# Selection rounds traced behind RWKV pairs, put-away tiles spread, the last two v tiles ordered by output block

## The chip, the cores and the metric

The kernel runs on one core of a Trainium2 chip. The metric is the device time of one execution in microseconds (us), lower is better. The core has five engines with instruction streams of their own: TensorE (PE, with its weight loads PEld), VectorE (DVE), ScalarE (ACT), GpSimd (POOL) and SyncE (SP), which issues most DMAs.

## The reference, cut to what matters

One layer over 384 tokens (128 sample tokens in 8 blocks of 16, and a prompt of 256), width 1024, float32:

```
x1 = norm and modulation of x, projected by W_in
rw = RWKV-7 over 16 heads        (kernel: 8 pairs of heads, R0 .. R7)
ix = sum over heads of relu(q_i . k_i) * w_i      (the indexer's scores)
keep = the 64 (prompt) best scores of each row; for the sample its own keys beside them
ds = attention over the kept keys only            (kernel: 4 quarters, D0 .. D3)
x2 = x1 + gated mix of rw and ds, through W_out
h  = norm of x2;  128 x 128 experts, 16 chosen for each of 8 heads
y  = x2 + gate * sum over chosen experts of  weight * gelu(h . u_e) * v_e
```

The expert layer at the end is done in two ways: the prompt's 256 tokens densely against all 16,384 experts, the 128 sample tokens by gathering the rows of the chosen experts only.

## The kernel before

The kernel is written on a tile framework. Instructions are traced in program order; a scheduler then sets the order on each engine from a simulated timeline, with the traced order as priority. Tiles come from pools by tag, each tag with a number of buffers; a tile waits for the release of the buffer that it takes, and a pool opened in space that another one held waits for all tiles of that one.

Front, up to about 740 us: the string ORDER (line 177) lists the units in traced order. I is the indexer, g and G gate units, R the RWKV pairs, D the attention quarters, M units of the modulation. For I, a pool "idx" is opened on the right side; `index` computes the indexer's projections and calls `index_s` (sample) and `index_p` (prompt, two tiles of 128 and 256 keys). Score tiles have the tag "isc" (2 buffers) in it. Their sums run on VectorE (L983, L987), after relu on ScalarE (L986, L1021). Then `select` runs its rounds on VectorE: 9 of them on 276 columns for the sample, 8 on 128 and 8 on 256 columns for the prompt, each a MAX8 (L964) and a MATCH_REPLACE8 (L965), and a mask is written (mks L1029 to L1034, mkp L992). When "idx" closes, the pool "dsa" is opened in its space (called ds); D, M and G units take their tiles from that, among them qx, the copy of a quarter's projections out of PSUM (L876). R units work in the pool "rw" (tags "y" and "sq2" among them).

Middle, 740 to 1330 us: the mix with W_out, the choice of experts, and the prompt's weights. G holds the weights of each expert tile's 128 experts for 256 tokens.

End: `dense_u(j)` multiplies the normed tokens by the u rows of expert tile j (in_puT), and writes gelu of it: the first 36 tiles with 8 products in full float32, the others with the operands split in high and low fp32r halves and 24 products. `dense_v(j)` reads the v rows (in_pv, 512 KB), splits them in a high and a low fp32r half (`split`: wh on ScalarE L227, wl on VectorE or GpSimd L231), weights the gelu tile on GpSimd (L1478), splits it likewise (Gh, Gl) and accumulates 12 products of 512 columns in four PSUM banks bx, cp, dx, dx (two token halves by two column halves). Every third tile is taken whole, without a split, except from n = 126 on. The u tiles are made ahead as far as there is room: 76 kept, 20 put away to DRAM (NB, tag gO, array Ad) and read back in `dense_v` (tag gB, L1472), 11 in buffers gA; the rest (21) are made inside the v loop, each as soon as fewer than 11 of the gA tiles are in use. The put-away tiles are j = 76 to 95. Meanwhile POOL issues 256 gathers (L1532) of u and v rows for the sample tokens, whose products VectorE sums. At the end `residual` multiplies each PSUM block by the gate (L1513) and adds x2 (L1514), then writes out.

Of the kernel before, what the change touches and what calls it, by code (L numbers as in the profile page):

```python
# [13 lines left out]
F32R = mybir.dt.float32r  # L14
# [159 lines left out]

PSB = {"mm": 2, "fx": 2, "bx": 1, "dx": 2, "cp": 1}
ALIAS = {"ix": "cp", "cs": "bx", "u": "fx"}
ORDER = "GGIggggRRDMMMGRMRDMRGMGMRMDGMMRRMGDMMMGGGMGGM"


N1, NW, NA, NB = 36, 76, 12, 20  # L180
SR, UR = (0.5, 0.4, 0.69), 0.5
S0, PH = 30, 4
WB, EB = (4, 4, 3), 5
UENG, VENG, GENG, VN = 'v', 'v', 'g', 3
SENG = 'gv'
# [7 lines left out]
class K:  # L193
# [684 lines left out]
    def index(self):  # L878
        nc = self.nc
        H = lambda t: t.rearrange("p i (h d) -> p i h d", d=64)  # L880
        kiT = self.t([128, NT], tag="kiT")
        W, n = self.win("ki")
        kt = self.t([72, NT], tag="kt")
        nc.scalar.activation(kt, self.tposp(W, 0, n, self.LT), AF.Copy)
        x = self.t([128, 3, 72], tag="qx")
        p = self.ps([128, 3, 72], tag="dx")
        for i in range(3):
            nc.tensor.transpose(p[:, i], kt[:, i * 128:(i + 1) * 128], self.ident[0:72, 0:72])
        nc.scalar.activation(x, p, AF.Copy)
# [12 lines left out]
        for u in range(2):  # L902
            x = self.t([128, 3, 256], tag="qx")
            self.nat3(f"qi{u}", x, 256)
            qr = self.t([128, 3, 4, 64], tag="qr")
            self.rope(qr, H(x), 0, 4)
            p = self.ps([128, 4, 128], tag="dx")
            for h in range(4):
                self.mm(p[:64, h], qr[:, 0, h], self.ident)
            nc.scalar.activation(qiTs[:, :, u * 4:u * 4 + 4].rearrange("p b h t -> p h b t"),  # L910
                                 p[:64].rearrange("p h (b t) -> p h b t", t=16), AF.Copy)
            p = self.ps([128, 2, 2, 128], tag="dx")
            for c in range(2):
                for i in range(2):
                    nc.tensor.transpose(p[:, c, i], qr[:, 1 + i, 2 * c:2 * c + 2].rearrange("p a b -> p (a b)"), self.ident)
            nc.scalar.activation(qiTp[:, u * 2:u * 2 + 2], p.rearrange("p c i t -> p c (i t)"), AF.Copy)
        self.mks = self.index_s(qiTs, kiT, wi[:, 0])
        self.mkp = self.index_p(qiTp, kiT, wi)

    def dsa_quarter(self, u):  # L920
        nc = self.nc
# [37 lines left out]
    def select(self, work, rounds):  # L959

        nc = self.nc
        for _ in range(rounds):
            m8 = self.t([128, 8], tag="m8", bufs=2)
            nc.vector.max(m8, work)  # L964
            nc.vector.match_replace(out=work, in_to_replace=m8, in_values=work, imm_value=MARK)  # L965

    def index_p(self, qiT, kiT, wi):
        nc = self.nc
        out = []
        for i in range(2):  # L970
            n = 128 * (i + 1)
            sc = self.t([128, 276], tag="isc", bufs=2)[:, :256]
            for par in range(2):
                pr = slice(64 * par, 64 * par + 64)
                for c0 in range(0, 4, 2):
# [11 lines left out]
                            nc.vector.scalar_tensor_tensor(sc[:, :n], rl[:, :n], w, sc[:, :n], op0=OP.mult, op1=OP.add)  # L987

            nc.vector.memset(sc[0:64, n - 64:n], -BIG)
            self.select(sc[:, :n], 8)  # L990
            mk = self.t([128, 256], BF16, tag="mkp", bufs=2, pool=self.hpool)
            nc.vector.tensor_scalar(mk[:, :n], sc[:, :n], MARK, -BIG, op0=OP.not_equal, op1=OP.mult)  # L992
            out.append(mk)
        return out

    def index_s(self, qiT, kiT, wi):
        nc = self.nc
# [14 lines left out]
        for b in range(8):  # L1012
# [3 lines left out]
            with self.tc.issue_after(self.wdma.ins):  # L1016
# [3 lines left out]
            rl = self.t([128, 272], tag="rel", bufs=2)  # L1020
            nc.scalar.activation(rl, p, AF.Relu)  # L1021
            self.mm(psc, LW[:, b].rearrange("p a b -> p (a b)"), rl, start=(b == 0), stop=(b == 7))
        sc = self.t([128, 276], tag="isc", bufs=2)
        nc.scalar.activation(sc[:, 0:272], psc, AF.Copy)

        nc.vector.memset(sc[:, 272:276], 3.0e38)
        self.select(sc, 9)
        mk = self.t([128, 384], BF16, tag="mks", pool=self.hpool)
        nc.vector.tensor_scalar(mk[:, 0:256], sc[:, 0:256], MARK, -BIG, op0=OP.not_equal, op1=OP.mult)  # L1029
        m2 = self.t([128, 16], tag="m2")  # L1030
        nc.vector.tensor_scalar(m2, sc[:, 256:272], MARK, -BIG, op0=OP.not_equal, op1=OP.mult)
        ob = self.t([128, 8], tag="ob8")
        nc.vector.tensor_scalar(ob, self.c["blk"], 1.0, BIG, op0=OP.subtract, op1=OP.mult)
        nc.vector.tensor_tensor(mk[:, 256:384].rearrange("p (b t) -> p b t", t=16), m2.unsqueeze(1).to_broadcast([128, 8, 16]),  # L1034
                                ob.unsqueeze(2).to_broadcast([128, 8, 16]), op=OP.min)
        return mk

    def attend_p(self, u, qT, kT, vn, obT):
        nc = self.nc
# [401 lines left out]
    def dense_u(self, j):  # L1441
# [8 lines left out]
        else:  # L1450
            uh, ul = (x.rearrange("p (k e) -> p k e", k=8) for x in self.split(u, UENG[j % len(UENG)]))
            hi, lo = self.h2p
            for k in range(8):
                self.mm(p, uh[:, k], hi[:, k], start=(k == 0), stop=False)
                self.mm(p, uh[:, k], lo[:, k], start=False, stop=False)
                self.mm(p, ul[:, k], hi[:, k], start=False, stop=(k == 7))
        off = NW <= j < NW + NB
        g = self.kept(j) if j < NW else self.t([128, 256], tag="gO" if off else "gA", bufs=2 if off else NA, pool=self.late)
        nc.scalar.activation(g, p, AF.Gelu_apprx_tanh)  # L1459
        if off:  # L1460
            nc.sync.dma_start(self.Ad[j - NW], g)
        return g

    def dense_v(self, j, g, out, n):
        nc = self.nc
        v = self.expert(self.I["pv"][j * 128:(j + 1) * 128])
        whole = n % VN == 0 and n < 126
        if not whole:
            vh, vl = self.split(v, VENG[j % len(VENG)])
        if NW <= j < NW + NB:  # L1470
            g = self.t([128, 256], tag="gB", bufs=2)
            nc.sync.dma_start(g, self.Ad[j - NW])  # L1472
        if j >= NW:
            q = (j - NW) % 4
            if q == 0 and j > NW:
# [3 lines left out]
        if whole:  # L1479
# [2 lines left out]
                    m = self.mm(out[i][b], g[:, i * 128:i * 128 + 128], v[:, b * 512:(b + 1) * 512], start=(n == 0), stop=False)  # L1482
            self.vdone.append(m.ins.name)
            return
        gh, gl = (self.t([128, 256], F32R, tag=tag, bufs=2) for tag in ("Gh", "Gl"))
        self.hilo(gh, gl, g, "v")
        for i in range(2):
            tok = slice(i * 128, i * 128 + 128)
            for q, (l, r) in enumerate(((gh, vh), (gh, vl), (gl, vh))):
                for b in range(2):  # L1490
                    m = self.mm(out[i][b], l[:, tok], r[:, b * 512:(b + 1) * 512], start=(n == 0 and q == 0),
                                stop=(n == 127 and q == 2))
        self.vdone.append(m.ins.name)

    def weights_back(self, j):

# [10 lines left out]
    def residual(self, i, parts, g, x1):  # L1507

        nc = self.nc
        y = self.ring()  # L1510
        for b in range(2):
            cols = slice(b * 512, b * 512 + 512)
            nc.vector.tensor_tensor(y[:, cols], parts[b], g[:, cols], op=OP.mult)  # L1513
            (nc.vector if i == 1 and b else nc.gpsimd).tensor_tensor(y[:, cols], y[:, cols], x1[:, cols], op=OP.add)  # L1514
            nc.sync.dma_start(self.O["y"][i * 128:(i + 1) * 128, cols], y[:, cols])

    def x1_rows(self, i):
# [40 lines left out]
    def run(self):  # L1558
        self.dense = False
        with ExitStack() as front:  # L1560
# [20 lines left out]
            with ExitStack() as s:  # L1581
                rw = self.open(s, "rw")
                self.pool = rw
                self.rwkv_head()
                ds, n = None, dict.fromkeys("RGD", 0) | {"M": 8}
                for x in ORDER:
                    if x == "I":
                        with ExitStack() as s2:
                            self.pool = self.open(s2, "idx", side="right")
                            self.index()  # L1590
                        ds = self.open(s, "dsa", side="right")
                        continue
                    self.pool = rw if x == "R" else ds
                    self.lo_pattern = "g" if x == "g" else "v"
# [39 lines left out]
                sn[0] -= 1  # L1634
                next(sparse, None)

        gs, todo = {}, list(range(NW, 128))
        for j in range(N1):
            self.dense_u(j)
            if j >= S0:  # L1640
# [10 lines left out]

        def ahead(n):
            un[0] += UR
            if todo and un[0] >= 1 and (todo[0] < NW + NB or todo[0] < NW + NB + NA - 1):
                un[0] -= 1
                u = todo.pop(0)
                gs[u] = self.dense_u(u)
# [13 lines left out]
        self.weights_back(NW)  # L1671
        self.g2 = self.modrow(5, "fx")

        self.vdone = []
        for n, j in enumerate(order):
            self.pace = self.vdone[n - 5] if n > 4 else None
            pull(SR[2])
            while todo and sum(u >= NW + NB for u in gs) < NA - 1:
                u = todo.pop(0)
                gs[u] = self.dense_u(u)  # L1680
            self.dense_v(j, gs.pop(j) if j >= NW else self.kept(j), out, n)
            if n == 122:
                for _ in sparse:
                    pass
                self.residual(0, [self.acc[:, b * 512:b * 512 + 512] for b in range(2)], self.gate2(0), self.x1_rows(0))
                g, x1 = self.gate2(1), [self.x1_rows(i) for i in (1, 2)]
        for i in range(2):
            self.residual(1 + i, out[i], g, x1[i])

# [24 lines left out]
```

## Time and profile before

| | us |
|---|---|
| median of 3 runs | 1815.54 (1814.88 to 1816.27) |
| profiled execution | 1820.84 |
| its span | 1819.1 |
| granted TensorE clock, mean | 0.969 |
| front (ORDER's units) | to about 740 |
| mix, choice, weights | about 740 to 1330 |
| v loop and its end | about 1330 to 1819 |

The profiled execution is one run and lies 5.3 us above the median. How its page is read: the busy rows show each engine's share in 40 slices of 45.5 us, in tenths; the row PEclk is the clock that TensorE was granted. A timeline row is start, duration, engine, line, operation, what it writes and reads, and in brackets the idle time ahead of it with what ended that.

### The profile page before, as it was taken

Reading aid. Unit: us, or ns where it says so; the run is one execution under the profiler, and the core shown is the slowest. Engines: PE = TensorE matmul, PEld = TensorE weight load, DVE = VectorE, ACT = ScalarE, POOL = GpSimd, SP = SyncE. Lnnn points to the kernel's source line nnn. Section 1 sums busy time; section 2 is a strip of 40 time slices with the busy share of each in tenths; the row PEclk is TensorE's granted clock in tenths of the full one; section 3 lists DMA queues with packets and bytes.
Section 4 is the critical chain, followed back from the end, with each engine's and each line's share of the span. In section 5 each row is a group of like instructions: output and inputs, shape, how many; then the busy total and the mean of one; then the engine's idle time right before and its main releaser. Section 6 shows DMA issues by size and latency. Waiting matters only on the chain. (4 is left out here: it accounts for less than half of the span.)

```text
span 1819.1 us, 33550 instructions
## 1 busy us (share of the span) xinstructions
PE 1722.2 (95%) x12576; PEld 1427.0 (78%) x12576; DVE 1353.9 (74%) x2942; ACT 701.7 (39%) x1411; POOL 687.8 (38%) x755
## 2 busy tenths in 40 slices
PE   6998899999999999999989999999998889999998
PEld 4986778877887877898878889999965556777765
DVE  3448867878677775455999999899957778777783
ACT  4532242333343333334322254488832223333332
POOL 1432232332233120024154446533355666555541
PEclk7998899999899998899999999999999999999999
DMA  8541373355354454655489989965489999999994
GB/s 289 161 129 44 90 255 114 102 172 159 118 193 133 124 198 164 226 181 170 151 326 327 339 312 364 380 236 184 170 303 379 393 366 374 347 382 355 341 342 150
DMA packets 181083, 434.11 MB, mean 239 GB/s; under 512 B 39348, under 2 KB 78388, under 8 KB 180920
## 3 DMA queue, kind: packets, MB, share of 16 engines
q1 hardware_dynamic: 144056, 297.73, 47.8%
q0 software_dynamic: 36864, 134.23, 19.8%
q8 instruction: 99, 1.62, 0.4%
q14 instruction: 64, 0.52, 0.1%
HBM read 401.65 MB, written 30.24 MB: 237 GB/s over the span
## 5 line engine op out<-in xcount | busy, mean ns | idle before, releaser
L231 DVE TENSOR_TENSOR wl<-w,wh 128x1024 fp32r<-128x1024 f32 (+1 forms) x274 | 343.9, 1258 | 140.3 <-ACT wh L227 77.2
L227 ACT ACTIVATE wh<-w 128x1024 fp32r<-128x1024 f32 (+1 forms) x282 | 296.0, 1053 | 203.9 <-PE mm L223 75.1
L1532 POOL DMA_INDIRECT raw<-in_pu,pe x128 | 162.4, 1269 | 173.2 <-PE dx L223 43.1
L223 PE MATMUL fx<-h2h,wh 128*128 128x256 f32 x736 | 215.4, 293 | 7.2 <-ACT wh L227 5.4
L223 PE MATMUL fx<-h2h,wl 128*128 128x256 f32 x736 | 212.3, 289 | 4.2 <-DVE wl L231 4.0
L1532 POOL DMA_INDIRECT raw<-in_pv,pe x128 | 168.8, 1319 | 124.1 <-PE dx L223 41.7
L223 PE MATMUL fx<-h2l,wh 128*128 128x256 f32 x736 | 209.3, 284 | 0.0
L1553 DVE SCALAR_TENSOR_TENSOR acc<-raw,dots,acc 128x1024 f32<-128x1024 f32 x127 | 164.9, 1298 | 10.5 <-DMA raw<-in_pv,pe 9.2
L1543 DVE SCALAR_TENSOR_TENSOR raw<-raw,sh 128x1024 f32<-128x1024 f32 x128 | 157.6, 1242 | 14.4 <-DMA raw<-in_pu,pe 14.2
L223 PEld LDWEIGHTS fx<-h2h,wh 128*128 128x128 f32 x736 | 139.9, 190 | 13.2 <-ACT wh L227 7.0
L223 PEld LDWEIGHTS fx<-h2h,wl 128*128 128x128 f32 x736 | 139.5, 190 | 7.7 <-DVE wl L231 5.9
L223 PEld LDWEIGHTS fx<-h2l,wh 128*128 128x128 f32 x736 | 140.0, 190 | 2.1 <-issue 1.7
L223 PE MATMUL fx<-h2f,w 128*128 128x256 f32 x576 | 128.6, 384 | 9.1 <-ACT G L1459 6.3
L223 PEld LDWEIGHTS fx<-h2f,w 128*128 128x128 f32 x576 | 109.8, 192 | 26.2 <-ACT G L1459 7.5
L223 PE MATMUL mm<-LTh,wh 128*128 128x384 f32 (+2 forms) x352 | 124.5, 354 | 1.6 <-ACT wh L227 1.0
L223 PE MATMUL mm<-LTh,wl 128*128 128x384 f32 (+2 forms) x352 | 123.2, 350 | 0.6 <-DVE wl L231 0.6
L223 PE MATMUL mm<-LTl,wh 128*128 128x384 f32 (+2 forms) x352 | 121.7, 346 | 1.1 <-POOL LTl L477 1.1
L223 PE MATMUL mm<-wh,LTh 128*128 128x256 f32 x336 | 99.1, 295 | 0.0
L223 PE MATMUL mm<-wl,LTh 128*128 128x256 f32 x336 | 98.3, 293 | 0.0
L223 PE MATMUL mm<-wh,LTl 128*128 128x256 f32 x336 | 98.1, 292 | 0.0
L1381 POOL TENSOR_TENSOR G<-G,wg 128x144 f32<-128x144 f32 (+1 forms) x64 | 54.4, 874 | 95.5 <-ACT wg L1378 95.5
L223 PEld LDWEIGHTS mm<-LTh,wh 128*128 128x128 f32 (+2 forms) x352 | 66.6, 189 | 10.1 <-issue 5.2
(557 smaller groups left out, 4157.5 us busy)
## 6 DMA issues: line engine op xcount, KB each, us to landing
w<-in_puT SPq DMA_DIRECT2D x128, 512.0 KB
w<-in_pv SPq DMA_DIRECT2D x128, 512.0 KB
w<-in_w_in SPq DMA_DIRECT2D x70, 512.0 KB
w<-in_w_ada SPq DMA_DIRECT2D x48, 512.0 KB
cKT<-in_cKT SPq DMA_DIRECT2D x32, 256.0 KB
cV<-in_cV SPq DMA_DIRECT2D x32, 256.0 KB
w<-in_w_pq SPq DMA_DIRECT2D x16, 512.0 KB
d<-wst SPq DMA_DIRECT2D x8, 832.0 KB
```

Of the source, the lines that this page charges most:

```text
L223: return self.nc.tensor.matmul(out, l, r, start=start, stop=stop, skip_group_check=True, **kw)
L227: self.nc.scalar.activation(hi, src, AF.Copy)
L231: (self.nc.vector if eng == "v" else self.nc.gpsimd).tensor_tensor(lo, src, hi, op=OP.subtract)
L1381: (nc.vector if w is p else nc.gpsimd).tensor_tensor(g, g, w[:, :, c0:c1], op=OP.mult)
L1532: d = nc.gpsimd.indirect_dma_start(out=u, out_offset=None, in_=src, in_offset=bass.IndirectOffsetOnAxis(ap=e[:, j:j + 1], axis=0))
L1543: nc.vector.scalar_tensor_tensor(u, u, 1.0, h2, op0=OP.mult, op1=OP.mult, accum_out=dots[:, j:j + 1])
L1553: nc.vector.scalar_tensor_tensor(acc, v, dots[:, j:j + 1], acc, op0=OP.mult, op1=OP.add)
```

## The change

It has three parts.

1. The rounds are no longer traced within `index_s` and `index_p` but in `pick_s` (sample), traced behind the first RWKV pair, and `pick_p` (prompt, one call per tile), both behind the second pair. Score tiles take buffers of the pool rw (tags "y" and "sq2") and the small tiles of the rounds (m8, m2, ob8) come from another pool, so that nothing of the rounds is left in the pool idx.
2. The 20 put-away tiles are spread over j = 76 to 127 (OFF) rather than the first 20 of them, and the 31 tiles made ahead (AHEAD) are those and the first 11 others. Gh and Gl have three buffers.
3. The products of the last two v tiles are made in `finish_v`, one output block after the other, with both tiles' products in each; the residual's adds of the prompt run on VectorE.

```diff
-ORDER = "GGIggggRRDMMMGRMRDMRGMGMRMDGMMRRMGDMMMGGGMGGM"
+ORDER = "GGIggggR1R23DMMMGRMRDMRGMGMRMDGMMRRMGDMMMGGGMGGM"
+OFF = [j for j in range(NW, 128) if (j - NW + 1) * NB // (128 - NW) > (j - NW) * NB // (128 - NW)]
+AHEAD = sorted(OFF + [j for j in range(NW, 128) if j not in OFF][:NA - 1])
+LAST = 126
...
-            m8 = self.t([128, 8], tag="m8", bufs=2)
+            m8 = self.t([128, 8], tag="m8", bufs=2, pool=self.hpool)
...
-            sc = self.t([128, 276], tag="isc", bufs=2)[:, :256]
+            sc = self.iscp[:, 128 * i:128 * i + n]
...
-            self.select(sc[:, :n], 8)
-            mk = self.t([128, 256], BF16, tag="mkp", bufs=2, pool=self.hpool)
...
+    def pick_p(self, i):
+        nc = self.nc
+        n, sc = 128 * (i + 1), self.isc[1 + i]
+        self.select(sc[:, :n], 8)
+        mk = self.t([128, 256], BF16, tag="mkp", bufs=2, pool=self.hpool)
+        nc.vector.tensor_scalar(mk[:, :n], sc[:, :n], MARK, -BIG, op0=OP.not_equal, op1=OP.mult)
+        self.mkp.append(mk)
...
-        sc = self.t([128, 276], tag="isc", bufs=2)
+        sc = self.t([128, 384], tag="y", pool=self.rw)[:, :276]
+        self.iscp = self.t([128, 384], tag="sq2", pool=self.rw)
...
+    def pick_s(self):
+        sc = self.isc[0]
         self.select(sc, 9)
...
-        off = NW <= j < NW + NB
+        off = j in OFF
...
-        whole = n % VN == 0 and n < 126
+        whole = n % VN == 0 and n < LAST
...
-        gh, gl = (self.t([128, 256], F32R, tag=tag, bufs=2) for tag in ("Gh", "Gl"))
+        gh, gl = (self.t([128, 256], F32R, tag=tag, bufs=3) for tag in ("Gh", "Gl"))
         self.hilo(gh, gl, g, "v")
+        if n >= LAST:
+            return gh, gl, vh, vl
...
+    def finish_v(self, parts, out):
+        prev = None
+        for i in range(2):
+            tok = slice(i * 128, i * 128 + 128)
+            for b in range(2):
+                for n, (gh, gl, vh, vl) in enumerate(parts):
+                    for q, (l, r) in enumerate(((gh, vh), (gh, vl), (gl, vh))):
+                        m = self.mm(out[i][b], l[:, tok], r[:, b * 512:(b + 1) * 512], start=False, stop=(n == len(parts) - 1 and q == 2))
+                        if prev is not None and n + q == 0:
+                            self.after(m, prev)
+                prev = m
...
-            (nc.vector if i == 1 and b else nc.gpsimd).tensor_tensor(y[:, cols], y[:, cols], x1[:, cols], op=OP.add)
+            (nc.vector if i else nc.gpsimd).tensor_tensor(y[:, cols], y[:, cols], x1[:, cols], op=OP.add)
...
-        gs, todo = {}, list(range(NW, 128))
+        gs, todo = {}, AHEAD + [j for j in range(NW, 128) if j not in AHEAD]
...
-            while todo and sum(u >= NW + NB for u in gs) < NA - 1:
+            while todo and sum(u not in OFF for u in gs) < NA - 1:
...
+        self.finish_v(last[LAST:], out)
```

How the engines' orders move is shown at three places. In the rows a name ends in a buffer's number, and the line numbers of the changed kernel are some higher.

ScalarE, at the end of the indexer, before: rel is the relu of the prompt's scores (L986), bn, kn, vn, sq, sig, ra, Di and cs belong to R0, qx to the quarter D0.

```order
L986 ACTIVATE rel_1105<-dx_1102 128x256
L621 ACTIVATE bn_1520<-fx_1521 128x384
L986 ACTIVATE rel_1108<-dx_1102 128x256
L621 ACTIVATE kn_1526<-fx_1527 128x384
L559 ACTIVATE sq_2007<-kk_2006 128x384
L621 ACTIVATE vn_1532<-fx_1533 128x384
L430 ACTIVATE sig_2002<-fx_2008,hb 128x384
L430 ACTIVATE ra_2003<-fx_2012,hb 128x384
L555 ACTIVATE Di_2005<-cs_2004 128x384
L554 ACTIVATE sig_2002<-sig_2002 128x384
L556 ACTIVATE cs_2004<-cs_2004 128x384
L876 ACTIVATE qx_2447<-mm_2460 128x256
```

The same place after the change (L989 is the relu, L879 the copy qx, L624 R0's copies):

```order
L989 ACTIVATE rel_1044<-dx_1041 128x256
L989 ACTIVATE rel_1047<-dx_1041 128x256
L879 ACTIVATE qx_2446<-mm_2459 128x256
L879 ACTIVATE qx_2446<-mm_2485 128x256
L230 ACTIVATE wh_2683<-w_2681 128x1024
L879 ACTIVATE qx_2446<-mm_2511 128x256
L230 ACTIVATE wh_2689<-w_2687 128x1024
L936 ACTIVATE rpt_2537<-qx_2446 128x768
L624 ACTIVATE bn_1433<-fx_1434 128x384
L624 ACTIVATE kn_1439<-fx_1440 128x384
L624 ACTIVATE vn_1445<-fx_1446 128x384
L562 ACTIVATE sq_1954<-kk_1953 128x384
```

D0's copies and its square stand ahead of R0's copies now, and right behind the last relu.

SP's queue at the start of the v loop, before: w from in_pv is a v tile, gB a readback, Ws the weights' readback.

```order
L1430 DMA w_15475<-in_pv 128x1024
L1384 DMA d_11262<-wst_15087 128x1664
L1430 DMA w_15487<-in_pv 128x1024
L1498 DMA Ws_15333<-d_11262 128x8x128
L407 DMA modr_15335<-d_102 128x1024
L1472 DMA gB_15449<-d_11263 128x256
L1472 DMA gB_15515<-d_11263 128x256
L1498 DMA Ws_15679<-d_11262 128x8x128
L1430 DMA w_15509<-in_pv 128x1024
```

After (w from in_puT is a u tile):

```order
L1442 DMA w_15472<-in_puT 128x1024
L1396 DMA d_11261<-wst_15083 128x1664
L1442 DMA w_15505<-in_pv 128x1024
L1525 DMA Ws_15332<-d_11261 128x8x128
L410 DMA modr_15334<-d_102 128x1024
L1484 DMA gB_15621<-d_11262 128x256
L1525 DMA Ws_15769<-d_11261 128x8x128
L1484 DMA gB_15868<-d_11262 128x256
L1442 DMA w_15517<-in_pv 128x1024
L411 DMA modr_15334<-in_b_ada 1x1024
L1442 DMA w_15539<-in_pv 128x1024
L1442 DMA w_15570<-in_puT 128x1024
```

u tiles are loaded between the first v tiles, where before the first 60 or so v tiles had none between them; one readback stands for about every sixth tile there, where two or three v tiles separated them before.

VectorE, its last rows, before:

```order
L231 TENSOR_TENSOR Gl_18843<-gA_18373,Gh_18842 128x256
L1513 TENSOR_TENSOR raw_18858<-bx_15329,raw_18747 128x512
L1513 TENSOR_TENSOR raw_18858<-cp_15330,raw_18747 128x512
L1513 TENSOR_TENSOR raw_18865<-dx_15331,raw_18747 128x512
L1513 TENSOR_TENSOR raw_18865<-dx_15332,raw_18747 128x512
L1514 TENSOR_TENSOR raw_18858<-raw_18858,raw_18754 128x512
```

and after:

```order
L234 TENSOR_TENSOR Gl_18830<-gB_18826,Gh_18829 128x256
L1540 TENSOR_TENSOR raw_18857<-bx_15328,raw_18742 128x512
L1541 TENSOR_TENSOR raw_18857<-raw_18857,raw_18749 128x512
L1540 TENSOR_TENSOR raw_18857<-cp_15329,raw_18742 128x512
L1541 TENSOR_TENSOR raw_18857<-raw_18857,raw_18749 128x512
L1540 TENSOR_TENSOR raw_18864<-dx_15330,raw_18742 128x512
L1541 TENSOR_TENSOR raw_18864<-raw_18864,raw_18751 128x512
```

The four multiplies stood in a row with one add behind them; now each is followed by its add, and one pair more stands behind the last row shown.

More of the change, by code (lines that the diff above doesn't have):

```diff
@@ L916, in index @@
             nc.scalar.activation(qiTp[:, u * 2:u * 2 + 2], p.rearrange("p c i t -> p c (i t)"), AF.Copy)
-        self.mks = self.index_s(qiTs, kiT, wi[:, 0])
-        self.mkp = self.index_p(qiTp, kiT, wi)
+        self.index_s(qiTs, kiT, wi[:, 0])
+        self.index_p(qiTp, kiT, wi)
     def dsa_quarter(self, u):
@@ L968, in index_p @@
         nc = self.nc
-        out = []
         for i in range(2):
             n = 128 * (i + 1)
-            sc = self.t([128, 276], tag="isc", bufs=2)[:, :256]
+            sc = self.iscp[:, 128 * i:128 * i + n]
+            self.isc.append(sc)
             for par in range(2):
@@ L989, in index_p @@
             nc.vector.memset(sc[0:64, n - 64:n], -BIG)
-            self.select(sc[:, :n], 8)
-            mk = self.t([128, 256], BF16, tag="mkp", bufs=2, pool=self.hpool)
-            nc.vector.tensor_scalar(mk[:, :n], sc[:, :n], MARK, -BIG, op0=OP.not_equal, op1=OP.mult)
-            out.append(mk)
-        return out
+    def pick_p(self, i):
[5 more added lines that the diff above has]
+        self.mkp.append(mk)
     def index_s(self, qiT, kiT, wi):
@@ L1022, in index_s @@
             self.mm(psc, LW[:, b].rearrange("p a b -> p (a b)"), rl, start=(b == 0), stop=(b == 7))
-        sc = self.t([128, 276], tag="isc", bufs=2)
+        sc = self.t([128, 384], tag="y", pool=self.rw)[:, :276]
+        self.iscp = self.t([128, 384], tag="sq2", pool=self.rw)
         nc.scalar.activation(sc[:, 0:272], psc, AF.Copy)
         nc.vector.memset(sc[:, 272:276], 3.0e38)
+        self.isc = [sc]
+        self.mkp = []
+    def pick_s(self):
+        nc = self.nc
+        sc = self.isc[0]
         self.select(sc, 9)
@@ L1029, in index_s @@
         nc.vector.tensor_scalar(mk[:, 0:256], sc[:, 0:256], MARK, -BIG, op0=OP.not_equal, op1=OP.mult)
-        m2 = self.t([128, 16], tag="m2")
+        m2 = self.t([128, 16], tag="m2", pool=self.hpool)
         nc.vector.tensor_scalar(m2, sc[:, 256:272], MARK, -BIG, op0=OP.not_equal, op1=OP.mult)
-        ob = self.t([128, 8], tag="ob8")
+        ob = self.t([128, 8], tag="ob8", pool=self.hpool)
         nc.vector.tensor_scalar(ob, self.c["blk"], 1.0, BIG, op0=OP.subtract, op1=OP.mult)
@@ L1035, in index_s @@
                                 ob.unsqueeze(2).to_broadcast([128, 8, 16]), op=OP.min)
-        return mk
+        self.mks = mk
     def attend_p(self, u, qT, kT, vn, obT):
@@ L1460, in dense_u @@
         if off:
-            nc.sync.dma_start(self.Ad[j - NW], g)
+            nc.sync.dma_start(self.Ad[OFF.index(j)], g)
         return g
@@ L1466, in dense_v @@
         v = self.expert(self.I["pv"][j * 128:(j + 1) * 128])
-        whole = n % VN == 0 and n < 126
+        whole = n % VN == 0 and n < LAST
         if not whole:
             vh, vl = self.split(v, VENG[j % len(VENG)])
-        if NW <= j < NW + NB:
+        if j in OFF:
             g = self.t([128, 256], tag="gB", bufs=2)
-            nc.sync.dma_start(g, self.Ad[j - NW])
+            nc.sync.dma_start(g, self.Ad[OFF.index(j)])
         if j >= NW:
@@ L1491, in dense_v @@
                     m = self.mm(out[i][b], l[:, tok], r[:, b * 512:(b + 1) * 512], start=(n == 0 and q == 0),
-                                stop=(n == 127 and q == 2))
+                                stop=False)
         self.vdone.append(m.ins.name)
+    def finish_v(self, parts, out):
[9 more added lines that the diff above has]
+                prev = m
     def weights_back(self, j):
@@ L1584, in run @@
                 self.rwkv_head()
+                self.rw = rw
                 ds, n = None, dict.fromkeys("RGD", 0) | {"M": 8}
@@ L1591, in run @@
                         ds = self.open(s, "dsa", side="right")
+                        continue
+                    if x in "123":
+                        self.pick_s() if x == "1" else self.pick_p("23".index(x))
                         continue
@@ L1653, in ahead @@
             un[0] += UR
-            if todo and un[0] >= 1 and (todo[0] < NW + NB or todo[0] < NW + NB + NA - 1):
+            if todo and un[0] >= 1 and todo[0] in AHEAD:
                 un[0] -= 1
@@ L1672, in run @@
         self.g2 = self.modrow(5, "fx")
-        self.vdone = []
+        self.vdone, last = [], []
         for n, j in enumerate(order):
@@ L1677, in run @@
             pull(SR[2])
-            while todo and sum(u >= NW + NB for u in gs) < NA - 1:
+            while todo and sum(u not in OFF for u in gs) < NA - 1:
                 u = todo.pop(0)
                 gs[u] = self.dense_u(u)
-            self.dense_v(j, gs.pop(j) if j >= NW else self.kept(j), out, n)
+            last.append(self.dense_v(j, gs.pop(j) if j >= NW else self.kept(j), out, n))
             if n == 122:
```

## The prediction

> **What bounds the kernel now.** I read the page's busy times and slices first, to see which engine the time belongs to and where it does not get its work.
>
> ```profile
> span 1819.1 us, 33550 instructions
> PE 1722.2 (95%) x12576; PEld 1427.0 (78%) x12576; DVE 1353.9 (74%) x2942; ACT 701.7 (39%) x1411; POOL 687.8 (38%) x755
> ...
> PE   6998899999999999999989999999998889999998
> ...
> PEclk7998899999899998899999999999999999999999
> DMA  8541373355354454655489989965489999999994
> ```
>
> TensorE is busy 95% of the span, so an edit pays only where that row is under 9 or the clock row is low. A slice is 45.5 us. The change touches three such places: slices 4 and 5 (about 137 to 227 us, both rows 8), the slices 30 to 32 (1319 to 1455 us, three 8s while DMA shows 9s), and the last one. The first place, in windows:
>
> ```profile
> core 0: us, PE busy (x) PEld busy (x) DVE busy (x) ACT busy (x) POOL busy (x), PEclk, DMA share, GB/s
> 150.00:160.00 10.00, 10.00 (x67) 8.54 (x65) 8.41 (x24) 1.50 (x3) 2.27 (x8) 1.00 0.22 75
> 160.00:170.00 10.00, 9.02 (x51) 5.85 (x51) 8.56 (x32) 1.70 (x5) 0.73 (x1) 0.74 0.18 31
> 170.00:180.00 10.00, 6.65 (x22) 4.13 (x21) 8.79 (x44) 4.97 (x11) 1.83 (x2) 0.50 0.03 7
> 180.00:190.00 10.00, 3.30 (x12) 2.70 (x13) 10.00 (x37) 0.00 (x0) 1.01 (x4) 0.50 0.00 1
> 190.00:200.00 10.00, 9.58 (x59) 7.68 (x57) 8.29 (x20) 2.91 (x5) 0.95 (x3) 0.72 0.59 167
> ```
>
> From 160 to 200 us TensorE idles 0.98 + 3.35 + 6.70 + 0.42 = 11.45 us, and its granted clock falls to 0.50. Who keeps it waiting is in the timelines of ScalarE and VectorE there:
>
> ```profile
> 164.29 0.66 ACT L986 ACTIVATE rel<-dx 128x256 f32<-128x256 f32 x2 [11.11 <-DVE isc L983]
> ...
> 178.93 0.51 ACT L556 ACTIVATE cs<-cs 128x384 f32<-128x384 f32 x1
> 191.39 0.66 ACT L876 ACTIVATE qx<-mm 128x256 f32<-128x256 f32 x2 [11.95 <-DVE mkp L992]
> ```
>
> ```profile
> 172.49 0.47 DVE L987 SCALAR_TENSOR_TENSOR isc<-rel,wi,isc 128x256 f32<-128x256 f32 x1
> ...
> 191.08 0.27 DVE L992 TENSOR_SCALAR mkp<-isc 128x256 bf16<-128x256 f32 x1
> ```
>
> The copy qx of the first attention quarter takes space that the index pool held, and that pool is released only when the last rounds' mask mkp is written, at 191.35. The last score sum was done at 172.96. The projections D0 may not leave PSUM until then; so PE has the chain of R0 alone.
>
> **Part 1, the rounds.** They are not made fewer or shorter: 25 pairs of maximum and replace stay on VectorE, at the same place in its order (behind the copy sq<-rk, as before). What changes is the release. Score tiles sit in the RWKV pool, m8, m2 and ob8 in another, so the index pool is free after the last sum, 172.96, less some us, since ScalarE's new order has all scores' relus ahead of R0's transposes and the qx copies right behind them. K0, Q0 and V0 products then fill the hole. If the hole closed and the clock stayed full, the gain would be the idle 11.45 plus the low clock: 9.02 × 0.26 + 6.65 × 0.50 + 3.30 × 0.50 + 9.58 × 0.28 = 10.0 us, 21.5 together. That is the upper bound. It isn't all to be had, because VectorE is the next to be late: in these 50 us it is busy 44.05, leaving 6 us, and it now gets what it did after 200:
>
> ```profile
> 201.30 0.94 DVE L935 TENSOR_REDUCE qss<-rpt 128x12 f32<-128x768 f32 x1
> ...
> 207.45 0.96 DVE L937 TENSOR_TENSOR qx<-qx,qss 128x768 f32<-128x768 f32 x1 [0.42 <-POOL qss L425]
> 208.44 0.96 DVE L868 TENSOR_TENSOR qr<-qx,rt 128x768 f32<-128x768 f32 x1
> ...
> 211.50 1.24 DVE L869 TENSOR_TENSOR qr<-qr,rpt 128x768 f32<-128x768 f32 x1
> ```
>
> ```profile
> L231 DVE TENSOR_TENSOR wl<-w,wh 128x1024 fp32r<-128x1024 f32 x3 | 3.7, 1225 | 1.0 <-PE mm L223 1.0
> ```
>
> One norm with its rotation is 0.94 + 0.96 + 0.96 + 1.24 = 4.1 us; the quarter has two, 8.2, and three weight splits at 1.225 go with its products, 3.7. Of these 11.9 us the spare 6 take half, and the rounds end some 6 to 8 us later beside R0's chain. So 21.5 − 8 = 13 (rounded down) is my value. The low end is −5: every engine's order from here to the mix at 740 us is drawn anew, and one dip more of the kind that stands there already, for example
>
> ```profile
> 720.00:740.00 20.00, 18.58 (x66) 14.87 (x66) 8.25 (x15) 5.45 (x14) 0.80 (x1) 0.54 0.58 200
> ```
>
> costs 1.42 idle and 18.58 × 0.46 = 8.5 of clock at worst, half of it where it is shorter: 5. New waits: R0's y waits for the sample's mask, its sq2 for the last prompt rounds. The tile view has the first write of y, ahead of that of sq2, at 247.2 us:
>
> ```profile
> L800 ACT ACTIVATE y<-cp x8: 383/383/384, 247.2 to 712.4; 128x256 f32<-128x256 f32 x8
> ```
>
> That is 56 us behind the last mask of today, so these waits cost nothing, even with rounds that end 8 us later and R0 13 us earlier.
>
> The Trainium skill, "TensorE: Matmul & The Clock Gate", Part 1 on the clock gate, has the array's clock halved after a stretch of too little work; the 0.50 in the two thin windows agrees, and by that rule the clock part of 10.0 us is won whole only if the hole closes to short gaps.
>
> **Part 2, put-away results spread, other u tiles pulled forward.** The stage that multiplies by the v tiles, in windows:
>
> ```profile
> 1340.00:1540.00 200.00, 178.07 (x625) 115.99 (x624) 151.42 (x196) 52.06 (x83) 128.82 (x109) 0.97 1.00 376
> 1540.00:1740.00 200.00, 197.07 (x968) 150.27 (x967) 154.80 (x191) 73.35 (x113) 107.95 (x84) 1.00 0.96 358
> 1740.00:1780.00 40.00, 40.00 (x140) 25.93 (x139) 30.21 (x36) 14.13 (x22) 14.71 (x11) 1.00 0.90 327
> ```
>
> The first half is bound by DMA (share 1.00, PE idle 22 us), the second by PE (197 of 200). The DMA view says why, of both halves:
>
> ```profile
> DMA packets 29805, 75.24 MB, mean 376 GB/s; under 512 B 2513, under 2 KB 13065, under 8 KB 29795
> ...
> w<-in_pv SPq DMA_DIRECT2D x52, 512.0 KB
> ...
> gB<-d SPq DMA_DIRECT2D x18, 128.0 KB
> w<-in_puT SPq DMA_DIRECT2D x3, 512.0 KB
> ```
>
> ```profile
> DMA packets 22345, 71.70 MB, mean 358 GB/s; under 512 B 2181, under 2 KB 5253, under 8 KB 22333
> ...
> w<-in_puT SPq DMA_DIRECT2D x18, 512.0 KB
> ```
>
> All but three of the 21 remaining u tiles, which cost PE most per byte, come in the second half; 18 readbacks gB, which cost bytes alone, in the first. The change mixes them: u loads begin behind the first v loads and end about two thirds through, readbacks run to the end. Number and bytes stay: 75.24 + 71.70 = 146.9 MB, and PE's 178.07 + 197.07 = 375.1 us. Well mixed, the 400 us are bound by the larger of 375 (gain 25) and 146.9 MB at the 376 GB/s which the first half held, 391 (gain 9); at today's mean of 367 GB/s it is 400, gain 0. Three waits in the first half show what PE lacks:
>
> ```profile
> PEld bx L223 <- ACT wh L227: 15.2, 6, 5.0
> ...
> ACT Gh L227 <- POOL gB L1478: 38.2, 9, 7.4
> ...
> ACT wh L227 <- DMA w<-in_pv: 28.2, 12, 5.6
> ```
>
> ScalarE waits for v tiles, and for results read back and then weighted on GpSimd; with readbacks rarer per us and a third Gh and Gl buffer that second wait is shorter. I take 8, near the 9 of the measured rate, with a range of 0 to 16 (half way from 391 to 375, were more slices like the 406 GB/s that stand in this view).
>
> The Trainium skill, "Perfetto Trace Analysis", box behind the Roofline section, gives 358 GB/s as a core's share with both cores of a pair at work, and about 435 as the ceiling of a core alone. The 376 GB/s over 200 us lies above the share, so the share is no limit here; by 358 the 146.9 MB would take 410 us, the part would lose 10 and the sum be 1820.84 − 5.5, 1810 on the median's scale, which I give no chance of its own; by 435 they would take 338 and leave PE's 375 as the bound, a gain of 25 and 1775.
>
> **Part 3, the tail.**
>
> ```profile
> 1809.62 0.63 PE L223 MATMUL dx<-wh,Gl 128*128 128x512 f32 x2
> 1809.67 0.69 DVE L1513 TENSOR_TENSOR raw<-bx,raw 128x512 f32<-128x512 f32 x1 [4.38 <-PE bx L223]
> ...
> 1810.44 4.15 POOL L1514 TENSOR_TENSOR raw<-raw,raw 128x512 f32<-128x512 f32 x3 [35.01 <-DVE raw L1513]
> 1810.87 1.28 DVE L1513 TENSOR_TENSOR raw<-dx,raw 128x512 f32<-128x512 f32 x2
> ...
> 1812.07 1.40 DVE L1514 TENSOR_TENSOR raw<-raw,raw 128x512 f32<-128x512 f32 x1
> ```
>
> PE's last product ends at 1810.25, all four blocks at once; then four multiplies and three adds on GpSimd (4.15 us) end at 1814.59. With 24 products in order of blocks, three blocks are multiplied and added while PE still works, and behind 1810.25 come one multiply (0.64 to 0.69) and one add on VectorE. The add is shown once, at 1.40 beside GpSimd; a multiply of the same shape takes 0.69, and with GpSimd gone I take 0.7. End 1811.65 to 1812.35 against 1814.59: 2.2 to 2.9; 2.5 taken, 1.5 to 3.2 with the start of the last two tiles uncertain (both now need a readback or a weight just before).
>
> **Sum.** 13 + 8 + 2.5 = 23.5 on the profiled execution's own 1820.84 is 1797.3. That execution stands 5.3 above the median shown, 1815.54, so on the scale of medians the forecast is 1792.
>
> **Rivals.**
> (a) The stage stays bound by DMA at its mean rate, and spreading only moves the idle time. For it: both halves move 358 to 376 GB/s, with share 0.96 to 1.00. Against: in the second half PE was the bound, so DMA could wait. Gain 13 + 0 + 2.5: 1800.
> (b) VectorE keeps the hole: rounds, norm and splits together outlast R0, whose chain needs VectorE (TL, Xk) as well. For: its 10.00 of 10 from 180 to 190. Against: PE has K0 to V0 to work on meanwhile. Front gain 4.5 instead of 13: 1800.5.
> (c) Slower: with both bounds in every window, each v tile waits for a load queued behind a u load, and each u load for a buffer that PE frees late, so neither reaches its rate. The price is the rate: at 327 GB/s, as in 1740 to 1780, 146.9 MB take 449 us, 49 more, and the sum is 1815.5 + 49 − 15.5 = 1849. It decides from 415.5 us (354 GB/s), where it eats the other two gains.
> (d) The change does not do what it says: scheduler and pools bring the same hole (part 1 at 0) and (a) holds too. Then only the tail is left: 1813.
>
> **How the numbers follow.** Chances: forecast 0.57, (a) 0.21, (b) 0.13, (c) 0.04, (d) 0.05. The range is 1779 to 1808: low end from 21.5 + 12 + 3.0 = 36.5, high end from 5 + 1 + 1.5 = 7.5; it holds (a) and (b) and leaves (c) and (d) out, with the extremes of the forecast. A measurement of this kernel tells about 0.2%, 3.6 us, from no change. Faster by more: 0.91; within: 0.05 (d); slower: 0.04 (c).
>
> **What would show it.** Part 1: qx behind the last rel with no wait for mkp, PE over 9 of 10 and clock over 0.9 in the windows from 160 to 190, and R0 to R1 reaching the mix some 13 us earlier. Were VectorE at 10 of 10 with PE still under 7, (b) is right. Part 2: u loads and readbacks in both halves, PE busy alike in both, and the stage from the first v product to the last about 8 us shorter than before; a DMA share of 1.00 throughout with PE at 94% means (a). Part 3: alternating multiply and add on VectorE, the last add about 1.4 us after PE's end. What would make the whole wrong is a new stall between 200 and 740 us, where the order is drawn anew, as the windows there would show.

## The result

| | before | after | ratio (95% interval) |
|---|---|---|---|
| median of 14 runs each, us | 1815.62 (1809.43 to 1819.66) | 1803.55 (1794.75 to 1810.66) | 0.9921 (0.9907 to 0.9936) |
| profiled execution, us | 1820.84 | 1796.01 | |
| its span, us | 1819.1 | 1794.1 | |

The change makes the kernel 0.79% faster, 14.3 us by the ratio (11.6 to 16.9). Forecast were 23.5 us and a time of 1792, with a range of 1779 to 1808: the time lies in the range, the sign is right, and the gain is about six tenths of the forecast one. The two profiled executions stand 24.8 us apart, about twice the difference of the medians: the one of before lies 5.2 us above its median, the one of after 7.5 us below. Whoever compares these two traces alone finds 10 us of gain too much.

The page of the kernel after, its slices (TensorE busy, granted clock, DMA share):

```profile
span 1794.1 us, 33542 instructions
...
PE   6999899999999999999999989999999999999998
...
PEclk7999899999999999999999999999999999999999
DMA  8543652463365364665499989964579999999995
```

The 8s at slices 31 to 33 (1364 to 1501 us, in the first half of the v loop; the prediction counts them one too low) and at 4 are gone; one 8 is left in slice 5, with the clock row at 8 there, around the wait at 200 us shown below, and another in slice 24, between 1032 and 1076 us, in the middle, which the change does not touch; the kernel before has one in slice 21. The same windows as before around the hole:

```profile
core 0: us, PE busy (x) PEld busy (x) DVE busy (x) ACT busy (x) POOL busy (x), PEclk, DMA share, GB/s
...
160.00:170.00 10.00, 10.00 (x79) 7.99 (x77) 8.55 (x27) 3.51 (x5) 0.74 (x1) 1.00 0.82 232
170.00:180.00 10.00, 8.07 (x61) 6.39 (x57) 7.90 (x34) 2.83 (x7) 5.26 (x3) 1.00 0.14 43
180.00:190.00 10.00, 9.57 (x68) 9.57 (x69) 9.08 (x31) 4.18 (x10) 3.28 (x6) 0.83 0.31 94
190.00:200.00 10.00, 6.98 (x76) 5.88 (x75) 8.96 (x24) 1.75 (x5) 6.39 (x3) 1.00 0.42 107
```

Idle is 1.93 + 0.43 + 3.02 = 5.4 us and low clock 9.57 × 0.17 = 1.6, together 7.0 where 21.5 stood. VectorE is no longer full at 10.00 of 10. On ScalarE's timeline the copy qx stands right behind the last relu and waits 1.22 us for the last score sum, where it waited 11.95 us for mkp:

```profile
157.81 0.38 ACT L989 ACTIVATE rel<-dx 128x256 f32<-128x256 f32 x1 [2.01 <-DVE sq L990]
159.41 0.39 ACT L879 ACTIVATE qx<-mm 128x256 f32<-128x256 f32 x1 [1.22 <-DVE sq L990]
```

The last mask mkp is now written at 203.4 us, 12 us later than before, and no copy waits for it. The idle time of the last window is one wait of TensorE for VectorE's rotation qr:

```profile
199.55 0.85 PE L948 MATMUL dx<-cfirst,qr 128*128 128x128 f32 x6 [3.02 <-DVE qr L872]
```

The v loop in windows:

```profile
1325.00:1525.00 200.00, 194.06 (x861) 141.46 (x860) 158.81 (x194) 64.58 (x102) 123.53 (x102) 0.99 0.99 371
1525.00:1715.00 190.00, 181.07 (x742) 127.52 (x741) 155.35 (x187) 61.34 (x92) 112.26 (x90) 0.99 1.00 372
```

Both stretches look alike now: TensorE at 97% and 95%, DMA at 0.99 and 1.00, 371 and 372 GB/s. Before it was 89% and then 98.5%, at 376 and 358. The end, on the timeline:

```profile
1788.81 0.40 PE L226 MATMUL dx<-wh,Gl 128*128 128x512 f32 x1
1789.25 0.69 DVE L1540 TENSOR_TENSOR raw<-dx,raw 128x512 f32<-128x512 f32 x1
1789.97 0.69 DVE L1541 TENSOR_TENSOR raw<-raw,raw 128x512 f32<-128x512 f32 x1
```

The last add ends at 1790.66, 1.45 us behind the last product, where it was 4.34. The add on VectorE takes 0.69, not the 1.40 that it took beside GpSimd.

### The profile page after: what moved, and what is told of

Its sections match the earlier page's. It is cut to its first block, busy times and chain, and to the rows that moved or that the text cites. A ratio compares the mean times of both kernels' runs of the same rounds, so it can differ in the third digit from the quotient of the medians.

```text
span 1794.1 us, 33542 instructions
## 1 busy us (share of the span) xinstructions
PE 1714.5 (96%) x12576; PEld 1420.0 (79%) x12576; DVE 1362.0 (76%) x2945; ACT 703.2 (39%) x1411; POOL 700.5 (39%) x752
## 4 chain that ended last, share of the span: by engine, by line
PE 67%; DVE 15%; DMA 10%; issue 3%; ACT 2%; POOL 2%; SPq 0%; DVEq 0%; ACTq 0%; POOLq 0%
PE mm L226 24%; PE fx L226 15%; PE dx L226 12%; PE cp L226 8%; PE bx L226 7%; DVE raw L1570 2%; DMA w<-in_pv 2%; DVE wl L234 2%; DVE acc L1580 1%; DMA w<-in_w_ada 1%; DMA raw<-in_pv,pe 1%; DMA w<-in_w_in 1%; DMA w<-in_puT 1%; ACT wh L230 1%; DVE psi L1297 1%
## 5 line engine op out<-in xcount | busy, mean ns | idle before, releaser
L1559 POOL DMA_INDIRECT raw<-in_pu,pe x128 | 154.6, 1208 | 181.1 <-PE dx L226 56.0
L1559 POOL DMA_INDIRECT raw<-in_pv,pe x128 | 173.0, 1351 | 120.4 <-PE dx L226 44.9
L1570 DVE SCALAR_TENSOR_TENSOR raw<-raw,sh 128x1024 f32<-128x1024 f32 x128 | 161.8, 1274 | 12.5 <-DMA raw<-in_pu,pe 11.7
L226 PEld LDWEIGHTS fx<-h2h,wl 128*128 128x128 f32 x736 | 140.2, 191 | 10.7 <-DVE wl L234 10.1
L1471 ACT ACTIVATE G<-fx 128x256 f32<-128x256 f32 x76 | 28.8, 383 | 122.8 <-PE fx L226 116.6
```

The lines of the kernel that those rows point to most:

```text
L226: return self.nc.tensor.matmul(out, l, r, start=start, stop=stop, skip_group_check=True, **kw)
L1559: d = nc.gpsimd.indirect_dma_start(out=u, out_offset=None, in_=src, in_offset=bass.IndirectOffsetOnAxis(ap=e[:, j:j + 1], axis=0))
L1570: nc.vector.scalar_tensor_tensor(u, u, 1.0, h2, op0=OP.mult, op1=OP.mult, accum_out=dots[:, j:j + 1])
```

## The experiments

Of each run the median stands with its ratio to the kernel before on the same chip. 0.1% is 1.8 us.

**Each part alone, and the whole once more.** The parts are taken from the diff in the section on the change; the core of each:

```diff
@@ p1_rounds @@
-ORDER = "GGIggggRRDMMMGRMRDMRGMGMRMDGMMRRMGDMMMGGGMGGM"
+ORDER = "GGIggggR1R23DMMMGRMRDMRGMGMRMDGMMRRMGDMMMGGGMGGM"
@@ p2_spread @@
-        gs, todo = {}, list(range(NW, 128))
+        gs, todo = {}, AHEAD + [j for j in range(NW, 128) if j not in AHEAD]
@@ p3_tail @@
+        self.finish_v(last[LAST:], out)
```

Expected of part 1 alone:

> Only the first part of the change: rounds traced behind the RWKV pairs, scores in tiles of the RWKV pool. The forecast's step: 13 us less than the kernel before (5 less at the least), won between 160 and 200 us, and the high half of the second norm's tile (h2h) written about 13 us earlier than at 870.7 us. Rival (b): 4.5 us less, VectorE full and TensorE under 7 of 10 in those windows. Rival on the shortfall: the front gives its 13 us in every run and what is short of 23.5 us is short in the v loop.

Of part 2 alone:

> Only the second part: put-away tiles spread over j = 76 to 127, the other u tiles pulled into the first v tiles, three buffers of Gh and Gl. The forecast's step: 8 us less than before, won between the first product by a v tile and the last one (about 479 us before). Rival (a): no gain, the loop is bound by DMA at its mean rate of 367 GB/s whatever the order.

Of part 3 alone:

> Only the third part: the last two v tiles' products in order of output blocks, the prompt's adds on VectorE, two buffers of Gh and Gl as before. The forecast's step: 2.5 us less (1.5 to 3.2), the last add about 1.4 us behind the end of TensorE's last product, where it was 4.3 us before. Rival: with two buffers the last tile's Gh comes late and the gain is under 1 us.

Of the whole:

> The whole change once more, for a second profile. If the shortfall against 23.5 us is one of the v loop, its length from the first product to the last differs from that of the first profile (469.7 us) by some us, while the front (h2h at 857.5 us) is the same within 1 us. If it is one of the front, it is the front that differs. By the 14 runs the median should be 12 us less than before.

| | median, us | ratio (95%) | gain by ratio, us | forecast, us |
|---|---|---|---|---|
| before, 35 runs | 1816.17 | | | |
| p1_rounds | 1814.12 | 0.9992 (0.9973 to 1.0011) | 1.5 | 13 |
| p2_spread | 1811.81 | 0.9972 (0.9947 to 0.9997) | 5.1 | 8 |
| p3_tail | 1813.16 | 0.9975 (0.9955 to 0.9995) | 4.5 | 2.5 |
| all_again | 1802.82 | 0.9930 (0.9903 to 0.9957) | 12.7 | 23.5 |

The parts sum to 11.1 us, about the whole. The shortfall is mostly part 1: its interval, from a gain of 4.9 us to a loss of 2.0, leaves 13 out. Yet in its profile the front ends early: h2h, with which the middle closes, is written at 859.9 us where the profile of before has 870.7. The other profiles resolve this. p2_spread and p3_tail have the old front, and h2h at 868.5 and 862.6; the whole change has 857.5 and 863.9. So executions of one and the same front differ by 6 to 8 us, and the profile of before was a late one. Over all profiles of whole kernels in this study the mean is 867.3 for the old front (three executions) and 860.9 for the new (six, two of them with a further edit in the front). With so few executions these 6 us do not settle it against the 1.5 us of the runs.

**The front without the v loop.** To time the front without the loop's spread, both orders with the loop cut to six tiles:

```diff
-        for n, j in enumerate(order):
+        for n, j in enumerate(order[:6]):
...
-            if n == 122:
-                for _ in sparse:
-                    pass
+            if n == 3:
```

> The kernel before, with the v loop cut to its first 6 tiles (the other 122, their u tiles and the rest of the sample's gathers are left out), so that nearly only the part ahead of the v loop is timed. About 1335 + 20 us by the trace. It stands beside cut_p1, the same cut with part 1.

> Part 1 alone with the same cut. If the front really ends earlier in every run and the v loop gives it back, this is 7 to 13 us under cut_before. If the hole of 160 to 200 us only moves to other dips of the front, it is within 3 us of cut_before, as part 1 alone was of the whole kernel before (1.5 us less).

Medians of 1366.56 us (ratio 0.7534, 0.7515 to 0.7553) and 1366.41 (0.7518, 0.7504 to 0.7532). By the medians the front gains nothing, by the ratios 2.9 us with intervals that overlap: the second case of the expectation, that the hole moves. In good part it does. The windows of the cut kernel with the old front, columns as above:

```profile
160.00:180.00 20.00, 12.11 (x49) 7.49 (x48) 18.85 (x81) 6.78 (x16) 3.56 (x6) 0.59 0.08 13
180.00:200.00 20.00, 16.45 (x118) 13.62 (x119) 15.73 (x46) 3.91 (x7) 0.95 (x3) 0.72 0.51 134
200.00:220.00 20.00, 19.99 (x218) 17.74 (x217) 17.56 (x45) 8.58 (x20) 8.56 (x7) 1.00 0.22 69
300.00:320.00 20.00, 19.62 (x192) 15.81 (x192) 17.86 (x59) 7.52 (x19) 6.16 (x7) 1.00 0.05 9
320.00:340.00 20.00, 19.50 (x212) 17.02 (x211) 18.31 (x36) 6.54 (x17) 8.23 (x11) 1.00 0.38 122
...
500.00:520.00 20.00, 20.00 (x228) 16.49 (x231) 15.40 (x36) 6.11 (x19) 8.51 (x11) 1.00 0.35 90
```

and with part 1:

```profile
160.00:180.00 20.00, 18.72 (x141) 14.94 (x140) 16.21 (x61) 6.72 (x12) 5.64 (x5) 1.00 0.47 134
180.00:200.00 20.00, 16.37 (x140) 15.14 (x139) 18.04 (x52) 5.94 (x14) 10.56 (x9) 0.91 0.32 91
200.00:220.00 20.00, 19.00 (x101) 12.62 (x104) 13.71 (x35) 7.27 (x14) 0.43 (x2) 0.66 0.81 274
300.00:320.00 20.00, 18.42 (x193) 16.33 (x193) 17.99 (x51) 8.22 (x18) 8.20 (x5) 0.96 0.22 73
320.00:340.00 20.00, 19.41 (x238) 17.32 (x237) 15.75 (x30) 8.45 (x18) 6.55 (x7) 0.96 0.30 83
...
500.00:520.00 20.00, 17.48 (x191) 13.93 (x191) 10.13 (x19) 9.51 (x17) 1.21 (x3) 0.91 0.75 238
```

Idle time plus busy time × (1 − clock), as in the prediction: from 160 to 200 us 12.9 + 8.2 = 21.0 before and 1.3 + 5.1 = 6.4 with part 1, a gain of 14.6. From 200 to 220 the clock is now at 0.66, a loss of 7.5 where there was none; 300 to 340 costs 3.7 instead of 0.9; 500 to 520 costs 4.1 instead of 0. These three places give 7.5 + 2.8 + 4.1 = 14.4 us back. Other windows are better than before: 440 to 480 costs 0.2 instead of 3.7, and 220 to 300 nothing instead of 1.8. Over all windows of 20 us from 160 to 520 us the loss is 27.5 us with the old order and 22.4 with part 1 (23.7 in cut_p1_again), so 5.1 of the 14.6 us are left at 520. By h2h, written at 862.8 and 863.1, they are gone: the new order loses 2.0 us more ahead of 160 us and 1.7 more behind 520, differences of a size that executions of one order show too. In the profiles with the old front the loss from 160 to 220 lies at 21 to 25 us each time, in those with the new one at 9 to 15.

What stands at 200 us is VectorE. In all nine profiles with the released pool TensorE waits 3.0 to 3.6 us for the rotation qr there, 3.02 in the change and 3.01 in cut_p1, and in the 5 us behind that wait the granted clock is 0.50 to 0.68; it is back at 1.00 within some 20 us. No run takes that wait away, so that the low clock comes of it is likely and not shown.

**Where the rounds are traced, or only what they hold.** ORDER with the rounds right behind the indexer, all else as in the change:

```diff
-ORDER = "GGIggggR1R23DMMMGRMRDMRGMGMRMDGMMRRMGDMMMGGGMGGM"
+ORDER = "GGI123ggggRRDMMMGRMRDMRGMGMRMDGMMRRMGDMMMGGGMGGM"
```

> The whole change, but with the rounds traced right behind the indexer (ORDER with 123 behind I): only the buffers are as in the change, the index pool is free without the rounds. The forecast said that the rounds hardly move and the release is what counts: within 3 us of the whole change (1803). Rival: where the rounds are traced matters, rounds take VectorE ahead of the RWKV chain, and it is 5 us or more slower than the whole change.

1800.95 us, ratio 0.9936 (0.9912 to 0.9960): the same as the whole change within what is told apart. Its last mask is written at 205.3 us, in the change at 203.4. So, once the index pool is free of the rounds, the place at which they are traced, which the title names, makes no difference that the runs tell; what part 1 does at the hole comes of the release.

**The u tiles pulled at an even rate.** In the loop:

```diff
-            while todo and sum(u not in OFF for u in gs) < NA - 1:
+            while todo and sum(u not in OFF for u in gs) < NA - 1 and 28 * (21 - len(todo)) < 21 * (1 + sum(i >= NW and i not in OFF for i in order[:n])):
```

> The whole change, with the 21 u tiles of the v loop pulled at an even rate over 28 of its 32 steps rather than as fast as buffers come free (21 of 32 steps). If mixing is what the v loop gains from, the last third, where no u tile is left, gets work from the first two: 2 to 4 us less than the whole change. If DMA's rate sets the loop whatever the mix, within 2 us of it.

1800.31 us, ratio 0.9925 (0.9902 to 0.9948), against 0.9921 and 0.9930 for the whole change: no difference. Once the loop is mixed by two thirds, mixing it to the end gains nothing, as it would be if DMA's rate sets the loop.

**The dip at 500 us.** What is behind it in the profile of the change, on the timelines of ScalarE and TensorE and among the waits of SP's queue from 484 to 506 us (waited for: total, times, longest):

```profile
508.05 1.06 ACT L230 ACTIVATE wh<-w 128x1024 fp32r<-128x1024 f32 x1 [1.49 <-DMA w<-in_w_in]
```

```profile
509.16 0.44 PE L226 MATMUL mm<-LTh,wh 128*128 128x384 f32 x1 [1.40 <-ACT wh L230]
```

```profile
SPq L957 <- ACT vv L879: 8.2, 1, 8.2
```

SP stands 8.2 us at the store of a quarter's v, and the loads of w_in are queued behind it. So I let ScalarE issue that store, in the cut kernels of both orders and in a whole one (which has u_even's rate too):

```diff
-        nc.sync.dma_start(self.O["v"][:, cols].rearrange("(i p) c -> p i c", p=128), vn)
+        nc.scalar.dma_start(self.O["v"][:, cols].rearrange("(i p) c -> p i c", p=128), vn)
```

> cut_p1 with one DMA moved: the store of a quarter's v (out_v<-vv, L954) is issued by ScalarE, which writes vv, rather than by SP. In every profile with part 1, SP stands 8.2 us at this store from 487 to 496 us, the loads of w_in behind it go out at 504, and TensorE waits for their split at 509. If this is where the front gives part 1's gain back, the wait at 509 is gone and the whole is 3 to 7 us under cut_p1. If it is not, another dip takes its place and it is within 2 us.

> The same edit without part 1. SP stands 12.3 us at that store in the kernel before, but TensorE has no wait there that the profile lays on a load: within 2 us of cut_before if the store only hurts in the new order; 3 us or more faster if it hurts in both.

> cut_p1 once more, beside the two on the same chip: 1366 us as before, with the hole of 160 to 220 us closed and the dip at 500 to 510 us again.

> The whole change with even u tiles and with that store on ScalarE: if both hold, 4 to 8 us under the whole change's 1803, the fastest of all; if the dip only moves, within 2 us of u_even (1800).

| | median, us | ratio (95%) |
|---|---|---|
| cut_p1_again | 1363.89 | 0.7516 (0.7495 to 0.7538) |
| cut_p1_store | 1362.33 | 0.7505 (0.7484 to 0.7525) |
| cut_before_store | 1401.60 | 0.7719 (0.7696 to 0.7743) |
| even_store | 1803.63 | 0.9938 (0.9916 to 0.9960) |

My theory of the store falls: 1.6 us by the medians, with ratios whose intervals overlap, not 3 to 7. The windows of cut_p1_store:

```profile
400.00:420.00 20.00, 17.22 (x189) 13.30 (x188) 13.01 (x41) 6.62 (x21) 7.26 (x12) 1.00 0.50 150
480.00:500.00 20.00, 18.39 (x210) 16.27 (x207) 16.51 (x47) 5.03 (x14) 5.65 (x4) 1.00 0.36 108
500.00:520.00 20.00, 18.59 (x258) 14.46 (x257) 12.31 (x33) 11.20 (x22) 0.43 (x2) 1.00 0.80 269
```

The dip at 500 shrinks from 4.1 to 1.4 us, and two new ones of 2.8 and 1.6 stand at 400 and 480, where cut_p1 has none. In the order of before, the same one-line edit costs 35 us (by the medians of the cut kernels), and no forecast of mine had that. Its tile view, against that of cut_before, shows the last quarter late:

```profile
L876 ACT ACTIVATE vv<-mm x12: 364/384/386, 215.8 to 667.5; 128x256 f32<-128x256 f32 x12
```

```profile
L876 ACT ACTIVATE vv<-mm x12: 378/384/392, 215.0 to 643.7; 128x256 f32<-128x256 f32 x12
```

The scheduler places the last quarter's v 24 us later, at 667.5, and h2h follows at 888.4 rather than 862.8. That is all that this execution lost (1389.99 us, the fastest of its five, against 1366.14); the slower ones were not profiled. even_store, with both edits, stands 3.3 us above u_even, within their intervals: no version beats the change by more than its runs are apart.

## Why the prediction came out so

**Part 1: the step that failed is "So 21.5 − 8 = 13 (rounded down) is my value".** At the hole the mechanism was right: the release lets D0's projections in, qx no longer waits for mkp, and the waits for y and sq2 cost nothing. The 21.5 us were right for the place, too; 14.5 to 14.6 of them are won from 160 to 200 us. The 8 us for VectorE have their cause in the traces, the wait for qr at 200 us with the low clock behind it: with the window up to 220 us the gain at the place is 7.2 us in the cut kernels (21.0 to 13.8) and 12.5 in the two profiles of the whole ones (23.1 to 10.7).

What the sum put at nothing is the rest of the redrawn order. I held it to be a risk (the text has −5 as the low end, while the range counts part 1 with a gain of 5) where it is a cost: the dips at 300 to 340 and at 500 to 520 us take 2.8 + 4.1 us more than before. And "R0 13 us earlier" did not happen. The hole is filled with D0's work, and R0 comes behind it; its first y, at 247.2 us before, is written 30 us later:

```profile
L803 ACT ACTIVATE y<-cp x8: 379/384/391, 277.6 to 702.7; 128x256 f32<-128x256 f32 x8
```

In the other profiles with part 1 it is at 276 to 282 us, with the order of before at 243 to 247 (the kernels with the moved store left out). The last pair's y comes at 703 to 708 us with part 1 and at 704 to 712 without, where some 13 us were forecast. The term measures 1.5 us (a loss of 2.0 to a gain of 4.9) in the whole kernel and 0 to 3 us in the cut ones. Rival (b), priced at 4.5 us, was near in size and half right in its cause: TensorE waits for VectorE, but VectorE is not full there, at 9.08 and 8.96 of 10, and the hole does not stay. What opens the two later dips is not settled; the one stall that was followed, to an SP queue, was replaced by others when it was taken away.

That the profile of before was a late one does not explain the miss. From 160 to 200 us, in windows of 20 us, it loses 22.4 us, and p2_spread, p3_tail and cut_before, with the same front, lose 24.6, 22.5 and 21.0. Its window from 720 to 740 us, quoted in the prediction with a clock of 0.54, has 0.74 in p3_tail and cut_before, but there the front is some 8 us further on: over the 40 us from the last RWKV pair's y on, all four have a clock of 0.74.

**Part 2: 8 forecast, 5.1 measured (0.5 to 9.6), between the forecast and rival (a).** The u loads and readbacks are in both halves, TensorE is busy alike in both, as said. In windows of 190 to 200 us DMA's share is 0.97 to 1.00 in every profile with the spread, which was the mark of (a). What the rate is differs by execution: 371 and 372 GB/s in the profile of the change, but in that of p2_spread

```profile
1330.00:1530.00 200.00, 190.95 (x826) 137.79 (x827) 151.08 (x188) 63.35 (x100) 111.07 (x96) 0.98 0.98 359
1530.00:1730.00 200.00, 189.35 (x779) 132.58 (x778) 161.08 (x194) 62.65 (x96) 123.19 (x94) 0.99 0.98 368
```

359 and 368, under the mean of before. I had taken 376, the rate of the half with next to no u loads. At 364 the 146.9 MB take 404 us, at 371.5 they take 395: no gain in the one, 5 us in the other, about what was measured. u_even agrees that the mix is no limit any more.

The sign named for this part, the stage 8 us shorter, was seen. From the first product of a split v tile to the last product it is 478.5 us before and 469.7 in the change. Over all whole kernels profiled it is 478.5 to 482.0 us in the three without the spread, at 364 to 366 GB/s from 1330 to 1730 us, and 467.1 to 476.8 in the six with it, shorter the higher the rate: 476.8 at 364, 475.1 at 366, 467.1 at 378. At equal rates the spread is worth 3 to 5 us; what goes beyond that is the rate of the execution.

The Trainium skill, "Perfetto Trace Analysis", box behind the Roofline section, puts a lone core's ceiling at about 435 GB/s; no window of 190 to 200 us of the loop measured here holds more than 379 (release_only), with the share at 1.00, so TensorE's 375 us never became the bound, which that figure would allow.

**Part 3: 2.5 forecast, 4.5 measured (0.9 to 8.2).** The trace of p3_tail shows 1.45 us from the last product to the last add, as in the whole change: 2.9 us less than before, the upper end of my step's 2.2 to 2.9. One us more is won behind it, which I had left out: from the last add to the span's end it is 3.4 us instead of 4.5. Two buffers of Gh and Gl were enough for that.

**Rivals.** (c), the slower one, did not show: the loop's mean rate stays above 354 GB/s in every whole kernel profiled. (d) has part 1 near nothing, as it was measured, but not in its way: the hole is gone, and part 2's interval leaves (d)'s gain of 0 out, if narrowly.

That the time lies in the range is in part luck: part 1, at 1.5 us, is below the 5 us that the range's end allows it, and parts 2 and 3, at 5.1 and 4.5 against 1 and 1.5 there, make up for it.

## What to carry to other kernels

A hole in a stage that a scheduler orders as a whole can be worth less than its length: here 14.6 us were won at one place, 9.5 of them were given back net by 520 us, and what was left did not show in the runs. The forecast of such an edit should give the redrawn rest a cost of its own, and a kernel cut behind the stage tells it in a few runs. Two traces can stand 10 us further apart than their medians: before sums are made on a profile, it is to be set against its own median and against a second profile of the same order, and windows of two profiles are to be laid on the same work, not on the same time. The edit at the tail, with no other work behind it, is the one that kept its forecast gain.

## What was not expected of the hardware

The same order of instructions ran its front, up to h2h, in 862.6 to 870.7 us. Most of the difference lies from 440 to 480 us, where the four executions with the old front lose 7.0 (before), 6.8 (p2_spread), 1.9 (p3_tail) and 3.7 us (cut_before). In each TensorE waits 1.6 to 2.0 us there for one load of TT; in the 10 us behind that wait the granted clock was 0.59 and 0.50 in before, 0.61 and 0.50 in p2_spread, 0.66 and 1.00 in cut_before, and 1.00 throughout in p3_tail. The window behind it, in before and in p3_tail:

```profile
460.00:480.00 20.00, 19.14 (x161) 18.29 (x162) 9.73 (x22) 4.22 (x11) 4.16 (x10) 0.74 0.37 124
```

```profile
460.00:480.00 20.00, 20.00 (x224) 18.28 (x225) 11.13 (x22) 6.25 (x12) 5.78 (x9) 1.00 0.46 153
```

So one and the same short wait can cost its own 2 us or 7. DMA at a share of 0.98 to 1.00 moved between 359 and 378 GB/s in windows of 200 us of the same loop.
